# S5 parameters in one go at the beginning, and layer 0's S5 pieces issued from the second v product on

## The chip, the cores and the metric

The kernel runs on one core of a Trainium2 chip. The metric is the device time of one execution in microseconds (us); lower is better.

## The reference

A bidirectional encoder of two layers over a sequence of 512 tokens with 1024 channels. Each layer has three mixers that read one normed input `h`, a gated merge of them, and an MLP:

```python
for l in range(DEPTH):
    h = rmsnorm(x, g1)
    z = h @ w_in                    # 1024 -> all branches' columns
    ya = swish(g) * head_norm(retention_bidir(rotary(q), rotary(k), v))   # A: 4 heads
    yb = glu(gelu(s5_bidir(u)))     # B: 16 groups, 64 complex states, both directions
    yc = swish(g) * head_norm(gla_bidir(q, k, v, log_gate))               # C: 4 heads
    x += (sum of sigmoid(h @ w_m) * (y @ w_y)) @ w_out
    x += relu(rmsnorm(x) @ w1) ** 2 @ w2
```

The S5 branch is a diagonal complex state `s[n] = a * s[n-1] + b * u[n]` for each group and direction, with `a` and `b` worked out from learned Lambda, dt and B.

## The kernel before

Activations lie as 128 channels by 512 tokens. Weights come in chunks of 128x1024: a DMA brings `raw`, ScalarE copies the rounded part to `whi` (L111), VectorE subtracts for the rest, `wlo` (L112), and TensorE multiplies three times for each 128x128 block: `whi` by the activation's high part (L128), `whi` by its low part (L129), `wlo` by its high part (L130). For the v products the roles of the operands are exchanged (L393, L395, L397). A chunk is 24 matmuls of 512 columns or 48 of 256.

In layer 0 the program goes: u tiles, low-rank gate input `lrT` (L597 to L613), four q and k tiles of GLA (`zc`, L376), the four gates (`gla_gate`, L631 to L654: VectorE scans `cum`, ScalarE exponentials, GpSimd's small products `dec`), two v products of GLA, four rotary tiles of retention (`za`; GpSimd's product with the sine L747, VectorE's sum L749, TensorE's transposes L770), two v products of retention (centred at L758 and L759), and then the silu and gate tiles, 3 S5 pieces behind each. All of this is issued by generators. The foreground, `self.fg`, steps through the heads of GLA and retention behind each product; the background, `self.bg`, is stepped by `bg_steps`, which holds the new instructions behind given anchors (`issue_after`).

Instructions of each engine run in the order in which they stand in its queue, which a scheduling layer makes out of priorities (`hp`) and these anchors. An instruction that waits holds up everything behind it on its engine.

The S5 branch has three parts that matter here. `s5_params` works out, for all layers and directions at once, Lambda's exponentials and powers in some 185 small operations of 128x32 on GpSimd (L895 to L1010; the reciprocal L976 stands on VectorE). `s5_prep` fetches the tile `s5BC` with a DMA that GpSimd issues (L1021), builds the powers `s5V` (copied from the parameters at L1027 and L1028, doubled at L1092 to L1099), `s5Bb` (L1035 to L1037), `W` (L1056 to L1061), TensorE's small products `psK` (L1070), `s5X` (L1116 to L1118), and transposes it on TensorE (L1125). `s5_half` multiplies (L1163, L1212) and scans (L1182).

Of the kernel before, what the change touches and what calls it, by code (L numbers as in the profile page):

```python
# [40 lines left out]
class Hybrid:  # L41
# [181 lines left out]
    def run(self):  # L223
        nc, io = self.nc, self.io
        self.cst = self.one([P, 2432], "cst")
        xp = [self.sb.tile([P, 2, 512], F32, tag="xp", bufs=4, name=self.nm("xp")) for _ in range(KT // 2)]
        self.x = [xp[j // 2][:, j % 2, :] for j in range(KT)]
        self.chunk = 0
        self.pre = {}
        with self.hp(25000):  # L230
            nc.sync.dma_start(self.cst[:, C_SM:C_N], io["cst"][:, C_SM:])
            nc.sync.dma_start(self.x[0], io["xT"][:, 0, :])
            self.prefetch(0, 0, 2)
            nc.sync.dma_start(self.x[1], io["xT"][:, 1, :])
            nc.sync.dma_start(xp[1], io["xT"][:, 2:4, :])
            self.prefetch(0, 1, 2)
            for j in (2, 3):
                nc.sync.dma_start(xp[j], io["xT"][:, 2 * j:2 * j + 2, :])
            nc.sync.dma_start(self.cst[:, 0:C_MB], io["cst"][:, 0:C_MB])
        nc.sync.dma_start(self.cst[:, C_MB:C_SM], io["cst"][:, C_MB:C_SM])  # L240
        self.xsrc = [io["xT"][:, j, :] for j in range(KT)]
        self.sm = self.cst[:, C_SM:C_N]
        self.ident = self.cst[:, C_ID:C_ID + P]
        self.ones = self.cst[:, C_ONE:C_ONE + P]

        zero, warm = self.slot(s="warm"), self.ms()
        with self.hp(40000):
            nc.vector.memset(zero, 0.0)
            for _ in range(3):
                nc.tensor.matmul(warm, zero[:, 0:P], zero, start=True, stop=True)  # L250
        self.warm = lambda: nc.tensor.matmul(warm, zero[:, 0:P], zero, start=True, stop=True)
        accs, h = [], []
        with self.hp(35000):
            for j in range(KT):
                h.append(self.scaled_split(self.x[j], self.sm[:, SM_G1 + j:SM_G1 + j + 1]))
        with self.hp(30000):
            for j in range(KT):
                self.acc_sq(accs, self.x[j], j, nc.vector)
        self.params = self.s5_params()
        next(self.params)  # L260
        for l in range(self.depth):
            self.chunk = 0
            h, accs = self.layer(l, h, accs)
# [160 lines left out]
    def layer(self, l, h, acc):  # L424
        nc, io = self.nc, self.io
        r, R, _ = self.norm_stats(acc)
# [14 lines left out]
                        lst.append(d)  # L441
        with self.hp(8000):
            gl = [self.gla_gate(hd, lrT, qd[hd], kd[hd]) for hd in range(4)]
        G, gla_o, cv = [], [], []
        for hd in range(4):
            G.append(self.gla_work(hd, qd[hd], kd[hd], gl[hd], cv, gla_o))
        cv.append(self.v_tiles(l, h, r, lambda: None))
        self.fg(G[0])
        cv.append(self.v_tiles(l, h, r, lambda: self.fg(G[0], G[1])))
        self.fg(G[0], G[1])  # L450
        aq, ak, av, ret_o = [], [], [], []
        cs, sn = self.slot(s="cos"), self.slot(s="sin")
        with self.tc.issue_after(self.wdma.ins):
# [2 lines left out]
        for t, lst, gens in ((0, aq, (G[1], G[2])), (0, ak, (G[2], G[3])), (1, aq, (G[2], G[3])), (1, ak, (G[3],))):  # L456
            z = self.z_tile(l, h, R, "za")
            with self.hp(10000):
                lst.append(self.rotary(z, cs, sn))
            self.fg(*gens)  # L460
        if l == 0:
            with self.tc.issue_after(self.rot[0].ins), self.tc.issue_after(self.rot[1].ins):
                next(self.params, None)
        Q = [self.ret_work(t, aq, ak, av, ret_o) for t in range(2)]
        av += self.center(self.v_tiles(l, h, r, lambda: self.fg(Q[0])))
        self.fg(Q[0], Q[1])
        yb = []
        self.bg = self.s5_work(l, us, yb)
        n = 3 if l == 0 else 1

        def silu(*gens):
# [78 lines left out]
        self.bg = iter(())  # L550
        prep = []
        if l + 1 < self.depth:
            self.bg = (None for t in range(2) for _ in self.s5_prep(l + 1, t, prep))
        acc, hn = [], []
        for q in range(4):
            hid = []
# [457 lines left out]
    def s5_prep(self, l, t, res):  # L1014
# [34 lines left out]
        for d in range(2):  # L1049
            k0 = kb + d * 4  # L1050
            sl = slice(0, 5) if d == 0 else slice(4, None, -1)
            pb = [self.pw[:, ri, k0:k0 + 4, sl].unsqueeze(3).to_broadcast(sh) for ri in range(2)]
            cb = [C[:, ri, d * 4:d * 4 + 4, :].unsqueeze(2).to_broadcast(sh) for ri in range(2)]
            for ri in range(2):
                tw = self.part(sh, "w5t")
                e1.tensor_mul(w[d][ri], pb[0], cb[ri])  # L1056
                e1.tensor_mul(tw, pb[1], cb[1 - ri])
                if ri == 0:
                    e1.tensor_sub(w[d][0], w[d][0], tw)
                else:  # L1060
                    e1.scalar_tensor_tensor(f(w[d][1]), f(w[d][1]), -1.0, f(tw), ALU.mult, ALU.subtract)  # L1061
                yield
        psK = self.ms([P, 2, 64])
        for d in range(2):
            kw = 0 if d == 0 else 1
# [40 lines left out]
        for d in range(2):  # L1106
            k0 = kb + d * 4
            sh = [P, 4, 4, 16]
            sl = slice(3, None, -1) if d == 0 else slice(0, 4)
            pb = [self.pw[:, ri, k0:k0 + 4, sl].unsqueeze(3).to_broadcast(sh) for ri in range(2)]  # L1110
            bb = [Bb[:, ri, d * 4:d * 4 + 4, :].unsqueeze(2).to_broadcast(sh) for ri in range(2)]
            PT = self.slot(shape=(P, 2, 2, P), s="s5PT" + z)
            X = self.slot(shape=(P, 2, 4, 4, 16), s="s5X")
            tx = self.slot(shape=(P, 1, 4, 4, 16), s="s5tx")
            for ri in range(2):
                e1.tensor_mul(X[:, ri], pb[0], bb[ri])  # L1116
                e1.tensor_mul(tx[:, 0], pb[1], bb[1 - ri])
                (e1.tensor_sub if ri == 0 else e1.tensor_add)(X[:, ri], X[:, ri], tx[:, 0])  # L1118
            nc.scalar.copy(d8[:, d], self.r4[:, k0:k0 + 4].unsqueeze(2).to_broadcast([P, 4, P]))
            e2.memset(d8[:, d, :, 0 if d == 0 else P - 1], 0.0)  # L1120
            yield
            pst = self.ms([P, 2, 2, P])
            for ri in range(2):
                for h in range(2):
                    nc.tensor.transpose(pst[:, ri, h, :], X[:, ri, 2 * h:2 * h + 2].rearrange("p a b c -> p (a b c)"),  # L1125
                                        self.ident)
            nc.scalar.copy(PT, pst)
            PTs.append(PT)
            yield
        res.append((w, M, Vr, Vi, PTs, d8))  # L1130

    def bg_steps(self, n, *anchors):

        with ExitStack() as st:
            for a in (*anchors, self.pool):
                st.enter_context(self.tc.issue_after(a.ins))
            for _ in range(n):
                next(self.bg, None)

    def s5_work(self, l, us, yb):  # L1140

# [7 lines left out]
    def s5_half(self, l, t, uU, prep, yb):  # L1149
# [6 lines left out]
        for d in range(2):  # L1156
# [37 lines left out]
                for x in S:  # L1194
                    e2.memset(x[:, :, 0 if d == 0 else P - 1], 0.0)
            Sp.append(S)
            yield

        Y = self.slot(shape=(P, 4, P), s="s5Y")
        psm = self.ms([P, 4, P])  # L1200
# [154 lines left out]
```

## Time and profile before

| what | value |
|---|---|
| median of 3 runs | 1555.6 us (1554.44 to 1556.1) |
| the profiled execution's own time | 1557.27 us |
| its span, first to last instruction | 1555.3 us |
| TensorE busy in it | 1536.5 us, 99% |
| VectorE busy | 950.2 us, 61% |
| ScalarE busy | 560.7 us, 36% |
| GpSimd busy | 214.4 us, 14% |
| TensorE's mean granted clock | 0.997 of full speed |

The span is the time from the first to the last instruction of one profiled execution; the execution's own time is 2 us longer. The profiled execution is 0.1% above the median. Busy shares are averages over the whole span.

### The profile page before, as it was taken

To read this page: it belongs to the slowest core of one execution; us is meant where nothing else is said; L and a number is where in the kernel's file an instruction comes from. 1 tells how busy PE (TensorE), PEld (TensorE's weight loads), DVE (VectorE), ACT (ScalarE), POOL (GpSimd) and SP (SyncE) were. 2 spreads that over 40 slices of the span, in tenths; PEclk is the share of its full clock that TensorE was granted. 3 is DMA by queue.
4 is the path that set the end of the run, shared out by engine and by line. 5 is a ranking of instruction groups with operands and counts; after the bars stand their busy time and mean duration, and the time that the engine had idled before them with its cause. 6 is when DMAs were issued, how large, how long until landed. Compare 5 with 4: busy or idle time off the path is not lost.

```text
span 1555.3 us, 20304 instructions
## 1 busy us (share of the span) xinstructions
PE 1536.5 (99%) x7984; PEld 1284.0 (83%) x7984; DVE 950.2 (61%) x1570; ACT 560.7 (36%) x842; POOL 214.4 (14%) x319
## 2 busy tenths in 40 slices
PE   8999999999999999999999999999999999999998
PEld 6988877888888888888889888888888888888897
DVE  6878999745655757434558788594466534343352
ACT  4534243324443232423435333233343413233242
POOL 8225010232200000000101211123121000000001
PEclk9999999999999999999999999999999999999999
DMA  6623223233332314231435222233332332223221
GB/s 211 190 62 109 67 82 114 97 112 130 109 102 76 125 55 141 86 111 61 142 118 161 89 89 82 91 113 122 109 135 95 98 106 95 95 95 105 85 95 54
DMA packets 59342, 163.86 MB, mean 105 GB/s; under 512 B 10540, under 2 KB 15148, under 8 KB 59248
## 3 DMA queue, kind: packets, MB, share of 16 engines
q1 hardware_dynamic: 58784, 161.27, 31.5%
q8 instruction: 62, 1.02, 0.3%
q0 software_dynamic: 320, 1.05, 0.3%
q14 instruction: 32, 0.26, 0.1%
q10 hardware_dynamic: 144, 0.26, 0.0%
HBM read 147.64 MB, written 6.52 MB: 99 GB/s over the span
## 4 chain that ended last, share of the span: by engine, by line
PE 86%; DVE 8%; DMA 2%; POOL 1%; issue 1%; SPq 1%; ACT 0%; DVEq 0%; POOLq 0%; ACTq 0%
PE mm L128 26%; PE mm L129 26%; PE mm L130 26%; DVE wlo L112 1%; DMA rsw<-za 1%; PE mm L393 1%; PE mm L395 1%; PE mm L397 1%; SPq L746 1%; PE mm L307 1%; DMA xp<-xT 0%; PE m L1163 0%; PE ms L673 0%; POOL sp L895 0%; PE m L1212 0%
## 5 line engine op out<-in xcount | busy, mean ns | idle before, releaser
L128 PE MATMUL mm<-hh,whi 128*128 128x512 f32 x1136 | 446.4, 393 | 0.4 <-ACT v L406 0.4
L130 PE MATMUL mm<-hh,wlo 128*128 128x512 f32 x1136 | 444.1, 391 | 0.8 <-DVE wlo L112 0.8
L129 PE MATMUL mm<-hl,whi 128*128 128x512 f32 x1136 | 444.1, 391 | 0.0
L111 ACT CAST whi<-raw 128x1024 fp32r<-128x1024 f32 (+1 forms) x250 | 258.3, 1041 | 223.2 <-PE mm L130 161.0
L112 DVE TENSOR_TENSOR wlo<-raw,whi 128x1024 fp32r<-128x1024 f32 (+1 forms) x250 | 329.4, 1318 | 3.7 <-PE mm L129 2.5
L128 PEld LDWEIGHTS mm<-hh,whi 128*128 128x128 f32 x1136 | 213.7, 188 | 46.6 <-issue 1.8
L130 PEld LDWEIGHTS mm<-hh,wlo 128*128 128x128 f32 x1136 | 213.6, 188 | 45.7 <-DVE wlo L112 1.2
L129 PEld LDWEIGHTS mm<-hl,whi 128*128 128x128 f32 x1136 | 213.7, 188 | 45.0 <-issue 1.6
L129 PE MATMUL mm<-fl,whi 128*128 128x512 f32 x448 | 174.4, 390 | 0.0
L130 PE MATMUL mm<-fh,wlo 128*128 128x512 f32 x448 | 174.1, 389 | 0.0
L128 PE MATMUL mm<-fh,whi 128*128 128x512 f32 x448 | 173.5, 390 | 0.0
L576 DVE TENSOR_TENSOR x<-x,mm 128x512 f32<-128x512 f32 x56 | 38.5, 687 | 134.8 <-PE mm L130 134.8
L563 ACT ACTIVATE ht<-ht 128x512 f32<-128x512 f32 x64 | 40.4, 632 | 186.8 <-DVE ht L562 186.8
L562 DVE SCALAR_TENSOR_TENSOR ht<-mm,R 128x512 f32<-128x512 f32 x64 | 44.2, 690 | 103.5 <-PE mm L130 92.5
L213 POOL TENSOR_TENSOR acc<-acc,sq 128x512 f32<-128x512 f32 (+1 forms) x24 | 30.6, 1275 | 551.4 <-ACT sq L212 551.4
L128 PEld LDWEIGHTS mm<-fh,whi 128*128 128x128 f32 x448 | 84.1, 188 | 17.8
L130 PEld LDWEIGHTS mm<-fh,wlo 128*128 128x128 f32 x448 | 84.1, 188 | 17.5
L129 PEld LDWEIGHTS mm<-fl,whi 128*128 128x128 f32 x448 | 84.1, 188 | 17.3
L490 ACT ACTIVATE g<-g,cst 128x512 f32<-128x512 f32 x48 | 34.8, 724 | 163.0 <-DVE g L489 163.0
L117 DVE TENSOR_TENSOR fl<-ht,fh 128x512 fp32r<-128x512 f32 x64 | 44.3, 692 | 71.6 <-ACT fh L116 71.6
L489 DVE TENSOR_TENSOR g<-mm,R 128x512 f32<-128x512 f32 x48 | 33.0, 687 | 63.3 <-PE mm L130 63.3
L130 PE MATMUL mm<-y,wlo 128*128 128x512 f32 x160 | 62.7, 392 | 0.9 <-DVE wlo L112 0.9
(297 smaller groups left out, 2134.4 us busy)
## 6 DMA issues: line engine op xcount, KB each, us to landing
raw<-wst SPq DMA_DIRECT2D x254, 512.0 KB, 3.3
dup<-zc SPq DMA_DIRECT2D x32, 128.0 KB, 3.5
rsw<-za SPq DMA_DIRECT2D x32, 64.0 KB, 2.3
qfb<-za SPq DMA_DIRECT2D x16, 128.0 KB, 2.3
x<-xT SPq DMA_DIRECT2D x8, 256.0 KB, 3.7
xs<-x SPq DMA_DIRECT2D x8, 256.0 KB, 2.4
x<-xs SPq DMA_DIRECT2D x8, 256.0 KB, 3.8
xp<-xT SPq DMA_DIRECT2D x3, 512.0 KB, 8.9
```

Source lines behind the costliest of these rows:

```text
L111: nc.scalar.copy(hi[:, s], raw[:, s])
L112: nc.vector.tensor_sub(lo[:, s], raw[:, s], hi[:, s].bitcast(F32))
L117: self.nc.vector.tensor_sub(lo, src, hi.bitcast(F32))
L128: nc.tensor.matmul(ps, hi[:, o:o + P], a, start=first and k == 0, stop=False)
L129: nc.tensor.matmul(ps, hi[:, o:o + P], b, start=False, stop=False)
L130: self.mmi = nc.tensor.matmul(ps, lo[:, o:o + P], a, start=False, stop=last and k == n - 1)
L213: return (eng or (nc.vector if j == KT - 1 else nc.gpsimd)).tensor_add(accs[0], accs[0], t)
L489: ev = nc.vector.tensor_mul(g, ps, R)
L490: act = nc.scalar.activation(g, g, AF.Sigmoid, bias=self.smc(l, SM_BM, j))
L562: ev = nc.vector.scalar_tensor_tensor(t, ps, 0.0, R2, ALU.max, ALU.mult)
L563: act = nc.scalar.square(t, t)
L576: ev = nc.vector.tensor_add(self.x[j], self.x[j], ps)
```

## The change

The generator `s5_params` is run to its end at the start, where before its first half was issued there and its second half behind the four rotary tiles. The background of S5 is set up behind the gates, and in layer 0 one step of it is taken behind each foreground step from the second v product on, with TensorE's last matmul and GpSimd's last product of the gates as anchors. The step count behind silu and gate tiles stays 3, but a step that yields a true value, which stands where the next piece begins on TensorE, ends the round. Lines of the changed kernel are those of before plus 1 (L376 is L377), plus 5 (L640 to L1125 are L645 to L1130), or plus 7 (L1163, L1212 and L1226 are L1170, L1219 and L1233). The work is the same; no instruction of the computation is added or taken away.

```diff
--- before.py
+++ after.py
@@ -257,7 +257,8 @@
             for j in range(KT):
                 self.acc_sq(accs, self.x[j], j, nc.vector)
         self.params = self.s5_params()
-        next(self.params)
+        for _ in self.params:
+            pass
         for l in range(self.depth):
             self.chunk = 0
             h, accs = self.layer(l, h, accs)
@@ -441,13 +442,22 @@
                         lst.append(d)
         with self.hp(8000):
             gl = [self.gla_gate(hd, lrT, qd[hd], kd[hd]) for hd in range(4)]
+        yb = []
+        self.bg = self.s5_work(l, us, yb)
+        self.pool = gl[0][1]
+
+        def fg(*gens):
+            self.fg(*gens)
+            if l == 0:
+                self.bg_steps(1, self.mmi)
+
         G, gla_o, cv = [], [], []
         for hd in range(4):
             G.append(self.gla_work(hd, qd[hd], kd[hd], gl[hd], cv, gla_o))
         cv.append(self.v_tiles(l, h, r, lambda: None))
         self.fg(G[0])
-        cv.append(self.v_tiles(l, h, r, lambda: self.fg(G[0], G[1])))
-        self.fg(G[0], G[1])
+        cv.append(self.v_tiles(l, h, r, lambda: fg(G[0], G[1])))
+        fg(G[0], G[1])
         aq, ak, av, ret_o = [], [], [], []
         cs, sn = self.slot(s="cos"), self.slot(s="sin")
         with self.tc.issue_after(self.wdma.ins):
@@ -457,15 +467,10 @@
             z = self.z_tile(l, h, R, "za")
             with self.hp(10000):
                 lst.append(self.rotary(z, cs, sn))
-            self.fg(*gens)
-        if l == 0:
-            with self.tc.issue_after(self.rot[0].ins), self.tc.issue_after(self.rot[1].ins):
-                next(self.params, None)
+            fg(*gens)
         Q = [self.ret_work(t, aq, ak, av, ret_o) for t in range(2)]
-        av += self.center(self.v_tiles(l, h, r, lambda: self.fg(Q[0])))
-        self.fg(Q[0], Q[1])
-        yb = []
-        self.bg = self.s5_work(l, us, yb)
+        av += self.center(self.v_tiles(l, h, r, lambda: fg(Q[0])))
+        fg(Q[0], Q[1])
         n = 3 if l == 0 else 1
 
         def silu(*gens):
@@ -550,7 +555,7 @@
         self.bg = iter(())
         prep = []
         if l + 1 < self.depth:
-            self.bg = (None for t in range(2) for _ in self.s5_prep(l + 1, t, prep))
+            self.bg = (x for t in range(2) for x in self.s5_prep(l + 1, t, prep))
         acc, hn = [], []
         for q in range(4):
             hid = []
@@ -1059,7 +1064,7 @@
                     e1.tensor_sub(w[d][0], w[d][0], tw)
                 else:
                     e1.scalar_tensor_tensor(f(w[d][1]), f(w[d][1]), -1.0, f(tw), ALU.mult, ALU.subtract)
-                yield
+                yield d and ri
         psK = self.ms([P, 2, 64])
         for d in range(2):
             kw = 0 if d == 0 else 1
@@ -1118,7 +1123,7 @@
                 (e1.tensor_sub if ri == 0 else e1.tensor_add)(X[:, ri], X[:, ri], tx[:, 0])
             nc.scalar.copy(d8[:, d], self.r4[:, k0:k0 + 4].unsqueeze(2).to_broadcast([P, 4, P]))
             e2.memset(d8[:, d, :, 0 if d == 0 else P - 1], 0.0)
-            yield
+            yield 1
             pst = self.ms([P, 2, 2, P])
             for ri in range(2):
                 for h in range(2):
@@ -1126,16 +1131,18 @@
                                         self.ident)
             nc.scalar.copy(PT, pst)
             PTs.append(PT)
-            yield
+            yield d
         res.append((w, M, Vr, Vi, PTs, d8))
 
     def bg_steps(self, n, *anchors):
+
 
         with ExitStack() as st:
             for a in (*anchors, self.pool):
                 st.enter_context(self.tc.issue_after(a.ins))
             for _ in range(n):
-                next(self.bg, None)
+                if next(self.bg, None):
+                    break
 
     def s5_work(self, l, us, yb):
 
@@ -1194,7 +1201,7 @@
                 for x in S:
                     e2.memset(x[:, :, 0 if d == 0 else P - 1], 0.0)
             Sp.append(S)
-            yield
+            yield 1
 
         Y = self.slot(shape=(P, 4, P), s="s5Y")
         psm = self.ms([P, 4, P])
```

How this moves instructions is seen in the engines' queues. First VectorE, behind the low-rank input `lrT` in layer 0. `wlo_527` of before and `wlo_574` of the change are the same chunk, the sixth counted from 0 (chunk 5). Before:

```order
L610 TENSOR_TENSOR lrT_392<-lrt_394,lrT_392 32x512
L112 TENSOR_TENSOR wlo_527<-raw_524,whi_526 128x1024
L376 TENSOR_TENSOR zc_477<-mm_452,R_277 128x512
L640 SCALAR_TENSOR_TENSOR a_565<-ms_563,a_565 128x512
L642 SCALAR_TENSOR_TENSOR cum_571<-scm_401,a_565 64x512
L643 SCALAR_TENSOR_TENSOR cum_571<-scm_401,a_565 64x512
```

With the change:

```order
L615 TENSOR_TENSOR lrT_439<-lrt_441,lrT_439 32x512
L1032 COPY s5V_145_921<-cst 128x8
L1033 COPY s5V_146_922<-cst 128x8
L1098 TENSOR_TENSOR s5V_145_921<-s5V_145_921 128x8
L1097 TENSOR_TENSOR s5vt_1611<-s5V_146_922 128x8
L1103 TENSOR_TENSOR s5V_146_922<-s5V_146_922,s5V_145_921 128x8
L1099 TENSOR_TENSOR s5V_145_921<-s5V_145_921,s5vt_1611 128x8
L1102 TENSOR_TENSOR s5vt_1611<-s5V_145_921,s5V_146_922 128x8
L112 TENSOR_TENSOR wlo_574<-raw_571,whi_573 128x1024
L1098 TENSOR_TENSOR s5V_145_921<-s5V_145_921 128x8x2
```

Two copies from the parameters `cst` and five products of `s5V` now stand ahead of the chunk's `wlo`, and more of them follow behind it.

Second GpSimd, behind the end of the parameters' first part. Before, the gate's `dec` follows it directly:

```order
L926 TENSOR_TENSOR sp_179<-sp_179 128x32
L904 TENSOR_SCALAR sp_222<-sp_222 128x32
L904 TENSOR_SCALAR sp_179<-sp_179 128x32
L653 TENSOR_TENSOR dec_581<-a_565,e_96_574 64x3
L654 TENSOR_TENSOR dec_581<-a_565,e_96_574 64x3
L685 MEMSET st_841 64x128
L686 MEMSET st_841 64x128
```

With the change (`sp`, `pwt` and `cst` are tiles of the parameters):

```order
L1013 TENSOR_TENSOR pwt_279<-cst 128x64
L900 TENSOR_TENSOR sp_253<-sp_253 128x32 x2
L1015 TENSOR_TENSOR cst<-pwt_278,pwt_279 128x32x2
L1014 TENSOR_TENSOR cst<-pwt_278,pwt_279 128x32x2
L900 TENSOR_TENSOR cst<-sp_253,sp_222 128x32 x2
L658 TENSOR_TENSOR dec_628<-a_612,e_99_621 64x3
L659 TENSOR_TENSOR dec_628<-a_612,e_99_621 64x3
L1026 DMA s5BC_917<-s5bc 128x512
L690 MEMSET st_888 64x128
L691 MEMSET st_888 64x128
```

The rest of the parameters now stands ahead of `dec`, of which these are the last rows, and the DMA of `s5BC` (L1021 before) stands right behind `dec`. The copies of `s5V` on VectorE wait for the last of the powers `v4r`, `v4i` and `r4`, which is the 135th instruction of GpSimd's queue, counted from its start; before, the 101st and 102nd were the L926 products of which one is shown above.

Third VectorE in the second half of layer 0's S5, around the last transposes of `s5X`. Before:

```order
L1116 TENSOR_TENSOR s5X_2734<-cst,s5Bb_2402 128x256 x2
L117 TENSOR_TENSOR y_3466<-yb_2358,y_3465 128x512
L112 TENSOR_TENSOR wlo_2874<-raw_2871,whi_2873 128x1024
L502 TENSOR_TENSOR g_2590<-g_2590,mm_2801 128x512
L1118 TENSOR_TENSOR s5X_2734<-s5X_2734,s5tx_2735 128x256
L1117 TENSOR_TENSOR s5tx_2735<-cst,s5Bb_2402 128x256
L1118 TENSOR_TENSOR s5X_2734<-s5X_2734,s5tx_2735 128x256
L1169 TENSOR_TENSOR s5a_2815<-m_459_2784,s5V_392_2398 128x2x2x128
```

With the change:

```order
L1121 TENSOR_TENSOR s5X_2734<-cst,s5Bb_2402 128x256 x2
L117 TENSOR_TENSOR y_3466<-yb_2358,y_3465 128x512
L1123 TENSOR_TENSOR s5X_2734<-s5X_2734,s5tx_2735 128x256
L112 TENSOR_TENSOR wlo_2874<-raw_2871,whi_2873 128x1024
L507 TENSOR_TENSOR g_2590<-g_2590,mm_2801 128x512
L1122 TENSOR_TENSOR s5tx_2735<-cst,s5Bb_2402 128x256
L1123 TENSOR_TENSOR s5X_2734<-s5X_2734,s5tx_2735 128x256
L1176 TENSOR_TENSOR s5a_2815<-m_459_2784,s5V_387_2364 128x2x2x128
```

The sum L1118 (L1123 now) on the first half of `s5X` stood behind the chunk's `wlo_2874` and a gate's product, and now stands ahead of both.

## Rows read from the trace of the kernel before

**Rows 1.** Stretches: from:to, length, busy us of PE, PEld, DVE, ACT, POOL, TensorE's clock.
```profile
40.00:72.00 32.00, 32.00 (x223) 29.39 (x222) 25.18 (x30) 19.68 (x34) 6.75 (x12) 1.00 0.74 214
72.00:120.00 48.00, 48.00 (x335) 43.05 (x334) 39.34 (x88) 18.90 (x56) 11.26 (x18) 1.00 0.25 70
268.00:270.00 2.00, 2.00 (x7) 1.68 (x6) 2.00 (x5) 1.40 (x2) 0.00 (x0) 0.50 0.09 33
```

**Rows 2.** TensorE's waits from 40 to 300: total, times, longest.
```profile
PE ms L1125 <- DVE s5X L1118: 2.0, 1, 2.0
PE mm L130 <- DVE wlo L112: 1.7, 2, 0.9
PE ms L770 <- DVE za L749: 1.3, 1, 1.3
PE ms L809 <- DVE v L759: 0.7, 1, 0.7
PE ms L738 <- DVE ro L836: 0.6, 1, 0.6
```

**Rows 3.** Timeline of TensorE, start and duration: one of the waits on wlo.
```profile
247.18 0.39 PE L129 MATMUL mm<-y,whi 128*128 128x512 f32 x1
248.46 0.50 PE L130 MATMUL mm<-y,wlo 128*128 128x512 f32 x1 [0.90 <-DVE wlo L112]
```

**Rows 4.** Timeline of TensorE behind the last wait: two matmuls at the low clock.
```profile
269.21 0.63 PE L128 MATMUL mm<-hh,whi 128*128 128x512 f32 x1
269.64 0.63 PE L129 MATMUL mm<-hl,whi 128*128 128x512 f32 x1
```

**Rows 5.** Timeline of GpSimd in the parameters, both parts, and dec between them.
```profile
30.72 0.47 POOL L913 TENSOR_TENSOR sp<-sp 128x32 f32<-128x32 f32 x2
...
39.30 0.29 POOL L904 TENSOR_SCALAR sp<-sp 128x32 f32<-128x32 f32 x1
39.55 1.88 POOL L926 TENSOR_TENSOR sp<-sp 128x32 f32<-128x32 f32 x2
...
51.30 0.69 POOL L653 TENSOR_TENSOR dec<-a,e 64x3 f32<-64x3 f32 x1 [9.37 <-DVE dup L650]
52.06 1.07 POOL L654 TENSOR_TENSOR dec<-a,e 64x3 f32<-64x3 f32 x1
...
130.04 0.24 POOL L895 TENSOR_TENSOR sp<-sp 128x32 f32<-128x32 f32 x1
...
132.22 0.25 POOL L1007 TENSOR_TENSOR pwt<-cst 128x32 f32<-128x32 f32 x1
```

**Rows 6.** Timeline of VectorE: the chunk's wlo, a gate's sum and scan.
```profile
40.08 1.22 DVE L112 TENSOR_TENSOR wlo<-raw,whi 128x1024 fp32r<-128x1024 f32 x1
...
44.19 0.69 DVE L640 SCALAR_TENSOR_TENSOR a<-ms,a 128x512 f32<-128x512 f32 x1 [2.28 <-ACT a L639]
44.91 1.22 DVE L642 TENSOR_TENSOR_SCAN cum<-scm,a 64x512 f32<-64x512 f32 x1
```

**Rows 7.** Timeline of VectorE: operations of the S5 pieces, in their old place.
```profile
140.94 0.29 DVE L1035 TENSOR_TENSOR s5Bb<-s5BC,cst 128x128 f32<-128x128 f32 x1
...
141.75 0.49 DVE L1056 TENSOR_TENSOR W<-cst,s5BC 128x320 f32<-128x320 f32 x1
...
162.68 0.17 DVE L1092 TENSOR_TENSOR s5vt<-s5V 128x8 f32<-128x8 f32 x1
```

**Rows 8.** Timeline of TensorE: the first use of wlo in chunk 5, 6, 8.
```profile
46.82 0.39 PE L130 MATMUL mm<-hh,wlo 128*128 128x512 f32 x1
47.05 0.39 PE L128 MATMUL mm<-hh,whi 128*128 128x512 f32 x1
...
51.92 0.28 PE L395 MATMUL mm<-wlo,hh 128*128 128x256 f32 x1
...
64.49 0.28 PE L395 MATMUL mm<-wlo,hh 128*128 128x256 f32 x1
```

**Rows 9.** The tile s5BC, four DMAs: from issue to landing.
```profile
DMA to landing us min/median/max: 2.9/3.0/4.7
```

## The prediction

> **What bounds the kernel now.** I began with the table of busy times: TensorE is busy in 99% of the span, so only its few pauses can be given back, and every new one is paid. The busy time by stretches [rows 1] shows where none are: from 40 to 72 us TensorE is busy in 32.00 of 32.00 us, from 72 to 120 in 48.00 of 48.00. VectorE is busy in 25.18 and 39.34 us there, so it idles for 6.8 and 8.7 us; this is the room into which the change moves S5 work.
>
> Then TensorE's own waits [rows 2]: six of them between 40 and 300 us, 2.0 + 1.7 + 1.3 + 0.7 + 0.6 = 6.3 us, every one for VectorE. The reader should see that none is for a DMA or for GpSimd, though these stand one step further back. A pause costs somewhat more than its idle time: around one wait for a `wlo` the starts are 248.46 - 247.18 = 1.28 us apart [rows 3] where the normal spacing is 47.05 - 46.82 = 0.23 [rows 8], so 1.05 are lost where the wait says 0.90. With 0.15 for each of six, 0.9 more. Behind the last wait the clock is granted at half [rows 1], and the matmuls start 0.43 us apart [rows 4] instead of 0.23. Some eight of them make 8 x 0.20 = 1.6 us. So 6.3 + 0.9 + 1.6 = 8.8 us is what the change can win at most here. Everything behind 300 us keeps its order, but for one small operation of VectorE.
>
> **The change part by part.** The edits change no work, so the sum is of new pauses against old ones.
>
> *A first new wait, in chunk 5.* VectorE's queue now holds the copies of `s5V` and five products ahead of chunk 5's `wlo`. They need the powers that GpSimd writes with its 135th instruction; before, 100 were behind it when the 101st began at 39.55 us [rows 5]. So 35 are left. Their pace: 34 instructions in 39.30 - 30.72 = 8.58 us, 0.25 each, or 11 in 132.22 - 130.04 = 2.18 us, 0.20 each [rows 5]. Dependent products and plain ones are mixed in both, so I take the middle: the powers are there at 39.55 + 35 x 0.227 = 47.5 us (46.6 to 48.4). VectorE, which in the old trace began this `wlo` at 40.08 [rows 6], has by its queue nothing else to do until then. Seven small operations follow; one takes 0.17 us [rows 7], less where the next one overlaps it, so I put 0.14 on each, 1.0 in all, and the `wlo` takes 1.22 [rows 6]. It ends at 49.7 us. TensorE uses it at 46.82 [rows 8]. **Term 1: +2.9 us.** Lower end, at 0.20 and 0.1 each, 1.7. Upper end: the pair at 39.55 took 1.88 us instead of 0.5 while VectorE worked [rows 5]; three more such pairs would add 4.1 and give 7.
>
> *The rule that bears on this pace.* Those two products took 0.94 us each beside VectorE's operations, against 0.20 to 0.25 elsewhere [rows 5]. The Trainium skill's SBUF — State Buffer (Who interferes with whom) says that a VectorE instruction with two SBUF inputs contends with a GpSimd instruction that reads SBUF, and holds it up. By that rule GpSimd would run free while VectorE stands still for it, the pace would be the 0.20 of the quiet stretch, and term 1 would be 2.0 instead of 2.9, the sum 0.9 us lower. The trace agrees as to the slow pair, but 34 instructions at 0.25 with a largely idle VectorE keep me at the middle.
>
> *A second, in chunk 6.* Behind chunk 5's `wlo` stand 13 small `s5V` operations (1.8), a `zc` and a gate's sum at 0.7 each, two scans of 1.22 [rows 6], then chunk 6's `wlo`: 49.7 + 1.8 + 1.4 + 2.4 + 1.2 = 56.5 us. TensorE, 2.9 late, wants it at 51.92 [rows 8] + 2.9 = 54.8. **Term 2: +1.7 us.**
>
> *A third, in chunk 8.* GpSimd issues the DMA of `s5BC` right behind the gate's `dec`, and `dec` needs VectorE's difference behind the `zc` of chunk 6 (56.5 + 1.3 = 57.8) and two exponentials, which I put at an operation of VectorE each (0.65): 59.1. `dec` took 53.13 - 51.30 = 1.8 us [rows 5], so the DMA is issued at 60.9 and lands 3.0 later (2.9 to 4.7) [rows 9], at 63.9. VectorE holds the `s5Bb` products behind that wait, and behind these chunk 8's `wlo`: six of `s5Bb` at 0.2 from start to start, six of `W` at 0.4 (their durations are 0.29 and 0.49 [rows 7], with some overlap), a gate's sum 0.7, two scans 2.4, the `wlo` 1.2, in all 8 us: 71.9. TensorE wants it at 64.49 [rows 8] + 4.6 = 69.1. **Term 3: +2.8 us** (1.5 with a fast `dec`, 4.5 with a landing of 4.7).
>
> *Clock.* Three pauses of 2 to 3 us come where there were none; the one of 2.0 before went with a low clock. Behind the first, the wait in chunk 6 would cover it, since VectorE decides there. Behind the third it would cost 1.6. I take half, **+0.8**.
>
> *The later chunks.* The remaining products of `W` and `s5Bb`, about 4 us, fall into the stretch with 8.7 us of room [rows 1], and TensorE is 7.4 us later itself. I cost them at nothing; without that cover each us of VectorE is a us.
>
> *What is given back.* The `s5X` sums no longer stand behind a chunk's `wlo`: the 2.0 of L1125 and its clock go. VectorE no longer waits for parameters at 131 and 141, the rotary sum stands ahead of the chunk's `wlo`, and the small `s5V` operations of the first half lie a hundred us earlier: 1.3 and 0.6 go. The two waits for `wlo` lay behind work of the second half that now comes earlier: 1.7. Of the 0.7 at v's centring about half stays, as `psK` moves in between the two v halves; and one pause of some 0.5 at the S5 output products is likely to be new, as they come sooner behind their scans. **Returned: 8.8 - 0.4 - 0.5 = 7.9.**
>
> *Sum:* 2.9 + 1.7 + 2.8 + 0.8 - 7.9 = +0.3 us. On the profiled execution, 1557.3, this is 1557.6; on the median of 1555.6, 0.1% below it, **1555.9**.
>
> **The rivals.**
>
> *Faster: the early waits are short.* Term 1 at 1.7, a quick `dec` and no low clock make 1.7 + 1.7 + 1.5 = 4.9, and all 8.8 come back: -3.9, 1551.7 us. For it: GpSimd runs beside an idle VectorE. Against it: three terms must be at their low ends together.
>
> *Slower: the late waits stay.* VectorE gives up some 12 us of work between 130 and 270 us, but it still holds wide scans, products and every `wlo`; a wait removed may come back one chunk on. If only half of 8.8 returns, 7.4 + 0.8 - 4.4 = +3.8, 1559.4 us; with a second low clock 1561. It decides from a return below 5.1. For it: every wait of [rows 2] is for VectorE, and the change takes no work from it. Against it: in [rows 2] five places alone hold all.
>
> *Slower: GpSimd is held up.* At the upper end of term 1, 4 us more, the lateness is carried through chunks 6 and 8: +4.3, 1559.9 us; with the slow landing 1561.6. Against it: VectorE has nothing to hold GpSimd up with while it waits.
>
> *The change does nothing* is no case: the copies' place in the queue is certain, so some wait must come.
>
> **How the numbers follow.** A measurement of this kernel tells 0.2%, 3.1 us, from no change. The forecast, a wash within that, gets 0.42; the short early waits 0.25; late waits that stay 0.21, GpSimd held up 0.12. So faster 0.25, same 0.42, slower 0.33. The range must reach into both sides: down to 1550.5, the faster case with another us from a `wlo` that isn't late; up to 1563, the slower cases with a low clock more.
>
> **What would show it.** In the changed profile VectorE should idle from about 40 to 47.5 us for GpSimd, ahead of an `s5V` copy; TensorE should wait near 47 us for 2 to 4 us at L130, near 55 and near 69 at L395, and the windows from 40 to 72 should no longer be full. Around 265 there should be no wait at L1130 and no low clock. The transposes of `za` should not wait. Wrong would be: no early pause at all (the powers ready before 43), or the same five places waiting as before, or a pause of over 10 us in the first 100.

## The result, and the profile after

The changed kernel takes 1568.56 us (median of 4, 1566.66 to 1570.4), the kernel before 1555.35 (4 runs, 1554.44 to 1556.1): a recorded ratio of 1.0075, with a 95% interval of 1.0062 to 1.0088 (the two medians alone give 1.0085). It is 13 us slower, above the range of 1550.5 to 1563. The profiled execution of the change took 1566.66 us and is the fastest of its four; against the 1557.27 of before that is 9.4 us, and it is these that the trace can explain.

TensorE's waits in the changed kernel from 30 to 320 us, in the columns of [rows 2]:

```profile
PE mm L130 <- DVE wlo L112: 4.5, 1, 4.5
PE m L1219 <- DVE s5S L1198: 4.3, 2, 2.3
PE mm L394 <- ACT v L407: 4.0, 1, 4.0
PE mm L394 <- DVE za L377: 1.3, 1, 1.3
```

Not one of the five places of [rows 2] waits as before: L1125 (now L1130), L770, L809, L738 and the two waits at L130 near 225 and 247 us are gone. In their place stand 4.5, 4.0, 1.3 and, at the S5 output products L1219, 4.3 us in two waits.

The stretches that were full [rows 1], and three short ones, in the columns of that group:

```profile
40.00:72.00 32.00, 25.91 (x152) 22.44 (x151) 19.42 (x45) 9.38 (x15) 15.77 (x55) 0.95 0.53 147
72.00:120.00 48.00, 45.59 (x320) 41.06 (x321) 42.93 (x84) 25.09 (x58) 9.02 (x20) 0.96 0.35 105
50.00:55.00 5.00, 4.15 (x11) 3.30 (x12) 4.83 (x17) 0.00 (x0) 1.89 (x5) 0.66 0.36 82
75.00:80.00 5.00, 5.00 (x32) 5.00 (x31) 4.78 (x10) 4.51 (x8) 1.50 (x2) 0.66 0.85 270
222.00:226.00 4.00, 4.00 (x17) 2.99 (x18) 2.31 (x5) 2.14 (x3) 0.00 (x0) 0.58 0.35 131
```

From 40 to 72 us TensorE is busy in 25.91 us instead of 32.00, from 72 to 120 in 45.59 instead of 48.00. In the last three rows the granted clock is 0.58 to 0.66: part of each stretch ran at 1.2 GHz instead of 2.4, and each lies behind a pause of 2.3 to 4.5 us.

The first pause, on VectorE (start, duration, instruction, and in brackets the idle time ahead with what ended it):

```profile
38.73 0.83 DVE L615 TENSOR_TENSOR lrT<-lrt,lrT 32x512 fp32r<-32x512 f32 x1
47.97 0.19 DVE L1032 COPY s5V<-cst 128x8 f32<-128x8 f32 x1 [8.40 <-POOL cst L900]
...
49.45 1.34 DVE L112 TENSOR_TENSOR wlo<-raw,whi 128x1024 fp32r<-128x1024 f32 x1
...
66.48 0.29 DVE L1040 TENSOR_TENSOR s5Bb<-s5BC,cst 128x128 f32<-128x128 f32 x1 [3.59 <-DMA s5BC<-s5bc]
```

This is where the prediction looked: `lrT` at 38.73, then 8.40 us of nothing until GpSimd's powers let the copies of `s5V` go at 47.97, then the `wlo` of chunk 5 from 49.45 to 50.79. The same on TensorE:

```profile
45.99 0.39 PE L129 MATMUL mm<-hl,whi 128*128 128x512 f32 x1
50.85 0.50 PE L130 MATMUL mm<-hh,wlo 128*128 128x512 f32 x1 [4.47 <-DVE wlo L112]
...
51.97 0.63 PE L130 MATMUL mm<-hh,wlo 128*128 128x512 f32 x1
52.39 0.63 PE L128 MATMUL mm<-hh,whi 128*128 128x512 f32 x1
```

L130 starts 4.86 us behind L129 instead of 0.23, and the matmuls behind it are 0.42 us apart. The second pause is put down to ScalarE, whose queue the prediction hadn't followed; its timeline, TensorE's, and the row of GpSimd and the one of VectorE on which it hangs:

```profile
70.27 0.60 ACT L1047 COPY s5Bd<-s5Bb 64x128 f32<-64x128 f32 x2 [6.29 <-DVE s5Bb L1042]
72.58 0.21 ACT L651 ACTIVATE e<-cum 128x4 f32<-128x4 f32 x1 [1.71 <-DVE cum L648]
72.91 0.60 ACT L1047 COPY s5Bd<-s5Bb 64x128 f32<-64x128 f32 x2
73.52 0.84 ACT L407 ACTIVATE v<-mm,ny 128x256 f32<-128x256 f32 x2
```

```profile
69.92 0.48 PE L678 MATMUL ms<-dup,dup 64*128 64x128 f32 x2
74.41 0.39 PE L394 MATMUL mm<-whi,hh 128*128 128x256 f32 x1 [4.01 <-ACT v L407]
74.64 0.28 PE L396 MATMUL mm<-wlo,hh 128*128 128x256 f32 x1
```

```profile
62.29 0.77 POOL L1026 DMA_DIRECT2D s5BC<-s5bc  x1
```

```profile
73.19 1.22 DVE L112 TENSOR_TENSOR wlo<-raw,whi 128x1024 fp32r<-128x1024 f32 x1
```

ScalarE idles 6.29 us for `s5Bb`, which VectorE can't build before `s5BC` has landed (issued at 62.29, and 3.59 us of VectorE's waiting end at 66.48, above). The copies of `s5Bd` (L1047) and the gate's exponential stand in ScalarE's queue ahead of L407, which empties the v product's PSUM tile, and without that tile, free at 74.36, TensorE can't begin the next v product. But the `wlo` of the same chunk, chunk 8, stands behind the same DMA in VectorE's queue and ends at 73.19 + 1.22 = 74.41: by these rows, had ScalarE been in time, TensorE would have stopped one matmul later, at L396, until the same moment. The third kind of pause, at 220 us, on VectorE and TensorE:

```profile
220.53 0.69 DVE L1194 TENSOR_TENSOR s5e<-s5e,s5V 128x512 f32<-128x512 f32 x1 [1.17 <-POOL s5d L1125]
221.14 0.68 DVE L1198 TENSOR_TENSOR s5S<-s5a,s5b 128x508 f32<-128x508 f32 x1
```

```profile
219.25 0.40 PE L128 MATMUL mm<-hh,whi 128*128 128x512 f32 x1
221.97 0.70 PE L1219 MATMUL m<-s5S,W 64*64 64x128 f32 x8 [2.32 <-DVE s5S L1198]
...
223.62 0.63 PE L128 MATMUL mm<-hh,whi 128*128 128x512 f32 x1
```

The output products L1219 need `s5S` (L1198), for which VectorE itself has waited 1.17 us for GpSimd, and they are now only seven matmuls behind the first of their kind at 217. Before, 40 matmuls stood between the first and the next (L1212 there):

```profile
217.73 0.67 PE L1212 MATMUL m<-s5S,W 64*64 64x128 f32 x16
...
228.68 1.85 PE L1212 MATMUL m<-s5S,W 64*64 64x128 f32 x48
```

### The profile page after: what moved, and what is told of

Same layout as the page of the kernel before. It is cut to its first block, busy times and chain, and to the rows that moved or that the text cites. A ratio compares the mean times of both kernels' runs of the same rounds, so it can differ in the third digit from the quotient of the medians.

```text
span 1564.8 us, 20298 instructions
## 1 busy us (share of the span) xinstructions
PE 1539.8 (98%) x7984; PEld 1286.3 (82%) x7984; DVE 949.3 (61%) x1570; ACT 560.3 (36%) x842; POOL 206.2 (13%) x319
## 4 chain that ended last, share of the span: by engine, by line
PE 88%; DVE 6%; POOL 3%; DMA 1%; issue 1%; SPq 1%; ACT 0%; DVEq 0%; POOLq 0%; ACTq 0%
PE mm L128 26%; PE mm L129 26%; PE mm L130 26%; PE mm L394 1%; DVE wlo L112 1%; PE mm L398 1%; PE mm L396 1%; DMA rsw<-za 1%; PE mm L308 1%; POOL sp L917 1%; SPq L751 1%; PE ms L678 1%; PE m L1219 0%; PE m L1170 0%; PE ms L832 0%
## 5 line engine op out<-in xcount | busy, mean ns | idle before, releaser
L130 PE MATMUL mm<-hh,wlo 128*128 128x512 f32 x1136 | 444.6, 391 | 4.5 <-DVE wlo L112 4.5
L129 PE MATMUL mm<-hl,whi 128*128 128x512 f32 x1136 | 444.8, 392 | 0.0
L130 PEld LDWEIGHTS mm<-hh,wlo 128*128 128x128 f32 x1136 | 214.0, 188 | 49.9 <-DVE wlo L112 5.3
L129 PEld LDWEIGHTS mm<-hl,whi 128*128 128x128 f32 x1136 | 214.1, 188 | 45.0 <-issue 1.6
L129 PE MATMUL mm<-fl,whi 128*128 128x512 f32 x448 | 174.4, 390 | 0.0
L130 PE MATMUL mm<-fh,wlo 128*128 128x512 f32 x448 | 174.1, 389 | 0.0
L129 PEld LDWEIGHTS mm<-fl,whi 128*128 128x128 f32 x448 | 84.1, 188 | 17.5
L130 PEld LDWEIGHTS mm<-fh,wlo 128*128 128x128 f32 x448 | 84.1, 188 | 17.4
L128 PE MATMUL mm<-y,whi 128*128 128x512 f32 x160 | 62.7, 392 | 0.0
```

The costliest lines, as they stand in the source:

```text
L128: nc.tensor.matmul(ps, hi[:, o:o + P], a, start=first and k == 0, stop=False)
L129: nc.tensor.matmul(ps, hi[:, o:o + P], b, start=False, stop=False)
L130: self.mmi = nc.tensor.matmul(ps, lo[:, o:o + P], a, start=False, stop=last and k == n - 1)
```

## The experiments

The ratios below are to the kernel before, measured beside each run (medians of 1555.3 to 1556.2 us). Names in the edits are those of the changed kernel.

**e1_params: only the parameters in one go.**

```diff
 (kernel before)
         self.params = self.s5_params()
-        next(self.params)
+        for _ in self.params:
+            pass
```

> Only the first part of the change: the parameters run to their end at the beginning, S5's pieces stay behind the silu and gate tiles. Theory A (the loss comes from VectorE's and ScalarE's queues, where early S5 pieces wait for GpSimd's powers and for the DMA of s5BC): nothing of VectorE's stands behind the parameters early, so no pause of TensorE between 40 and 120 us, and the two waits of VectorE at 131 and 141 us go: 1553 to 1556 us. Theory B (the loss comes from GpSimd being busy with parameters when the gates' dec are due): slower than before, 1559 us or more.

1552.68 us, ratio 0.998 (0.997 to 0.9989). Theory B falls: the parameters that GpSimd now works out earlier are in nobody's way, and this part of the change wins 2.6 us. VectorE's waits from 120 to 150 us show it, first before, then here; those for the parameters at L976 and L1027 are gone:

```profile
DVE sp L976 <- POOL sp L895: 1.7, 1, 1.7
DVE s5V L1027 <- POOL cst L895: 1.6, 1, 1.6
```

```profile
DVE za L749 <- DMA rsw<-za: 2.8, 1, 2.8
```

**e2_nobreak: the change without the rule that ends a round.**

```diff
-                if next(self.bg, None):
-                    break
+                next(self.bg, None)
```

> The changed kernel without the rule that a piece that begins on TensorE ends the round of steps. Theory A: the early waits stay as they are, 1565 to 1570 us. Theory C (the loss is that the pieces now come out in smaller rounds, so that the S5 output products stand too close behind their scans and wait for them): these waits go, 1560 to 1564 us.

1564.39 us, ratio 1.0055 (1.0035 to 1.0076), between the two expectations. Both theories hold in part: the early pauses are there, and the long waits at the output products are not (none of them is over 0.3).

```profile
PE mm L130 <- DVE wlo L112: 5.0, 2, 3.6
PE mm L394 <- ACT v L407: 4.4, 1, 4.4
PE mm L396 <- DVE wlo L112: 1.7, 1, 1.7
```

**e4_anchor: the early steps behind the chunk's `wlo`.**

```diff
-                nc.vector.tensor_sub(lo[:, s], raw[:, s], hi[:, s].bitcast(F32))
+                self.wsub = nc.vector.tensor_sub(lo[:, s], raw[:, s], hi[:, s].bitcast(F32))
...
-                self.bg_steps(1, self.mmi)
+                self.bg_steps(1, self.mmi, self.wsub)
```

> The changed kernel, with VectorE's last wlo as one more anchor for the early single steps, so that VectorE's part of a piece stands behind the wlo of the chunk whose weights were last fetched; nothing else. The copies of s5V then stand behind the wlo of chunk 8 instead of ahead of that of chunk 5. Theory A: the pauses at 46 and 70 us go and their low clocks with them, 12 us less than the changed kernel by its profile: 1554 to 1559 us. Theories B and C: GpSimd's work and the rounds are the same, so 1565 us or more.

1559.86 us, ratio 1.0025 (1.0016 to 1.0035): 8.7 us less than the change, just above what theory A gave. The pause for the powers is gone and that at L394 down to 0.3, but new ones stand in the GLA heads, which I had not expected:

```profile
PE m L1219 <- DVE s5S L1198: 4.3, 2, 2.3
PE ms L702 <- DVE st L697: 3.8, 2, 2.5
PE ms L678 <- DVE sT L681: 1.4, 1, 1.4
PE mm L394 <- ACT v L407: 0.3, 1, 0.3
```

**e5_bcfirst: the change, with layer 0's first `s5BC` fetched at the beginning.**

```diff
+        self.bc0 = self.pslot(shape=(P, 2, 2, 8, 16), s="s5BC")
+        self.nc.gpsimd.dma_start(self.bc0, self.io["s5bc"][0, 0])
         self.params = self.s5_params()
...
```

In `s5_prep` this tile then takes the place of the one fetched there.

> The changed kernel, with the DMA of s5BC for layer 0's first half issued at the very beginning, ahead of the parameters. Theory A: the wait for the powers at 46 us stays with its low clock (6 us), the second at 70 us (4 us, and a low clock) goes: 1561 to 1565 us. If the second wait is ScalarE's own and not owed to s5BC: 1566 to 1570 us, with the wait for the v tile still there.

1563.56 us, ratio 1.0054 (1.0035 to 1.0072), 5.0 us less, as theory A says. The 4.0 at L394 has gone; 1.4 and 2.4 us at the GLA products L680 remain of that stretch.

**e6_anchor_nobreak: e4_anchor and e2_nobreak together.** Edit: both diffs.

> e4_anchor without the rule that ends a round ahead of a piece that begins on TensorE. Theory A (early S5 work of VectorE and ScalarE in front of the work that TensorE wants next, wherever it stands) leaves the waits of the GLA heads at 73, 81 and 110 us in place, 5 to 6 us; theory C in its part (the round ends bring the S5 output products too close behind their scans) takes the two waits of 2.3 and 2.0 us and a low clock away: 1554 to 1556.5 us. If the rounds don't matter: 1559 to 1561 us.

1558.72 us, ratio 1.0017 (1.0006 to 1.0028), 2 us above the expectation. The waits at the output products shrink from 4.3 to 0.3 us, those of the GLA heads stay (3.8 and 0.9), and a wait of 1.4 for a `wlo` near 207 us is new. Against e4_anchor only 1.1 us are won.

**e7_params_break: parameters and rule, no early steps.** Every `fg` of the change is `self.fg` again:

```diff
-        cv.append(self.v_tiles(l, h, r, lambda: fg(G[0], G[1])))
+        cv.append(self.v_tiles(l, h, r, lambda: self.fg(G[0], G[1])))
...
```

> Parameters in one go and the rule that ends a round, but no early steps: S5's pieces behind the silu and gate tiles, as before. Against e1_params (1552.7 us) it has the rule alone more. Theory C: the output products wait for their scans, 2 waits of 2 us: 1555 to 1558 us. If the rule only moves waits from one piece to another: 1551 to 1554 us.

1551.55 us, ratio 0.9976 (0.9965 to 0.9987). The rule alone costs nothing here: 1.1 us less than e1_params, within what the intervals allow, so the time that theory C gave is not reached. But a wait of its kind is there: one of 2.7 us at L1219 is nearly all that is left from 30 to 320 us:

```profile
PE m L1219 <- DVE s5S L1198: 2.7, 1, 2.7
```

**e8_late and e9_rotary: early steps that begin later, behind the `wlo`, without the rule.** The first steps stay `self.fg` up to the last v product (e8) or up to the first rotary tile (e9).

> Parameters in one go, early single steps only at the last v product (retention's), two of them, behind the chunk's wlo on VectorE, and rounds of 3 without the rule. Theory A: GLA's heads are through by then, so no wait of theirs; the late waits (223, 260, 286 us in e1_params, some 3 us) move or shrink: 1550 to 1553 us. If early pieces cost wherever they stand: 1554 us or more.

> As e8_late, but single steps from the first rotary tile on, six of them. Theory A: the pieces fall among the last GLA heads and hold their state products up, by part of the 6 us of e4_anchor: 1553 to 1557 us. If only the waits for parameters and s5BC count (both are over by then): 1550 to 1553 us.

1552.48 us, 0.9978 (0.9969 to 0.9987), and 1553.75 us, 0.9991 (0.9982 to 1.0001). With e1_params (no early step, 1552.68) and e6_anchor_nobreak (eight, from the second v product, 1558.72) they make a series. No difference among the first three is clear of the intervals, so late steps win nothing; the two steps that e6_anchor_nobreak has more than e9_rotary, ahead of the rotary tiles, cost 5.0 us.

**e10_gap: e7_params_break, with an empty round ahead of the output products.**

```diff
             Sp.append(S)
             yield 1
 
+        if l == 0:
+            yield 1
         Y = self.slot(shape=(P, 4, P), s="s5Y")
```

> e7_params_break with one empty round more in layer 0, between the last scan of an S5 half and its output products. In e7_params_break these products wait 2.7 us for their scans and a short low clock follows; theory C: a tile more in between hides the wait, 1547 to 1550 us. If the wait only moves to what now comes last: 1551 to 1553 us.

1549.02 us, ratio 0.996 (0.9945 to 0.9975), the fastest of all. The wait at the output products is gone, and the longest left is 0.7:

```profile
PE ms L775 <- DVE ny L144: 0.7, 1, 0.7
```

**e11_late_break: e8_late with the rule.** Edit: the rule of the change is kept.

> e8_late with the rule that ends a round. Without early steps the rule was worth 1 us (e7_params_break against e1_params), with eight early steps it cost 1 to 4. If two late single steps don't matter to it: 1550.5 to 1552.5 us. If the rule costs where pieces come earlier: 1553 us or more.

1552.2 us, ratio 0.998 (0.9971 to 0.999): no difference from e8_late. Without the steps ahead of the rotary tiles the rule is neutral.

**e12_moreparams: the change, with 20 more operations of GpSimd.**

```diff
         c = ts(cm, 1.0, ALU.add)
+        for _ in range(20):
+            e.tensor_scalar(c, c, 0.0, None, ALU.add)
         yield
```

> The changed kernel with 20 more small operations of GpSimd in the parameters, each of which adds zero. By this the scheduling layer puts the copies of s5V behind the wlo of chunks 5 and 6 instead of ahead of that of chunk 5. Theory A (the place in VectorE's queue decides): the pause at 46 us and its low clock go, though GpSimd has 4 to 5 us more to do; a shorter wait stays ahead of chunk 7, and the one at 70 us stays: 1561 to 1566 us. Theory B (GpSimd's time decides): 4 us slower than the changed kernel, 1570 us or more.

1566.62 us, ratio 1.0068 (1.0047 to 1.009). It is not the 4 us slower of theory B, and by the intervals no different from the change, but not as theory A said either. The copies stand behind two more chunks' `wlo`, and VectorE waits for the powers there instead, longer, and one pause of 9.0 us takes the place of two:

```profile
DVE s5V L1034 <- POOL cst L900: 10.9, 1, 10.9
```

```profile
PE mm L396 <- DVE wlo L112: 9.0, 1, 9.0
```

So the place decides which chunk is late, and GpSimd's time how long. Neither alone gives the size.

**e13_nowprod, e14_anchor_bcfirst, e15_bcfirst_nowprod: what holds the GLA heads up.** All three start from e6_anchor_nobreak. e13 leaves the `W` products of layer 0's first half out and sets `W` to zero, e14 fetches the first `s5BC` at the beginning (the diff of e5), e15 does both.

```diff
+                if kb == 0:
+                    e2.memset(w[d][ri], 0.0)
+                    yield d and ri
+                    continue
                 tw = self.part(sh, "w5t")
```

> e6_anchor_nobreak, with the W products of layer 0's first S5 half left out and W set to zero by GpSimd instead: 12 operations of VectorE of 0.4 us, 4.9 us, less, between 70 and 110 us. Theory A (VectorE's S5 work in front of the products of the GLA states is what TensorE waits for at 73, 81 and 110 us): these waits shrink from 4.7 us to under 2, 1554 to 1556.5 us. If those waits are owed to something else (GpSimd's memsets, the DMA of s5BC): 1558 to 1560 us.

> e6_anchor_nobreak (1558.7 us) with the DMA of s5BC for layer 0's first half issued at the very beginning; VectorE's order is the same. Theory D (VectorE's wait for that DMA, in front of the second gate's sum and scans, starts the lateness of the GLA heads): the wait of 1.8 us at 66 us goes and the waits at 73 to 123 us shrink by as much or more: 1555 to 1557 us. Theory E (the work of VectorE alone, 7 us of it in a stretch with 8.7 us of room, all told): 1558 to 1559.5 us.

> e14_anchor_bcfirst with the W products of the first half left out and W set to zero by GpSimd, so that neither the wait nor most of the work is left. Theories D and E together: the waits at 73 to 123 us go to under 1.5 us in all: 1552.5 to 1555 us. If a third thing holds the heads up: 1557 us or more.

1559.7 us (ratio 1.0028, 1.0016 to 1.0039), 1556.22 us (1.0001, 0.9992 to 1.001) and 1554.43 us (0.9982, 0.9973 to 0.9992). e13 missed: without the products the kernel is no faster. In its trace VectorE waits 3.4 us for `s5BC` where e6_anchor_nobreak waits 1.8, and the rotary tile `za` is later too, so a transfer and the work are mixed there. e14 answers to theory D, with 2.5 us won. With the wait gone the work shows: e15 wins another 1.8. TensorE's waits in the last two; in both, 0.8 at L680 stays:

```profile
PE ms L704 <- DVE st L699: 2.8, 2, 2.5
...
```

```profile
PE mm L130 <- DVE wlo L112: 1.4, 1, 1.4
PE mm L396 <- DVE za L379: 1.4, 1, 1.4
...
```

**e16_all: the change with the anchor, the early `s5BC` and the empty round.** Edit: the diffs of e4, e5 and e10.

> The change with three mends: VectorE's anchor, s5BC fetched at the beginning, and the empty round ahead of the output products. Against e10_gap (1549.0 us), which has the last and no early steps, it shows what early steps are worth when nothing of theirs waits: 1551 to 1555 us if VectorE's early work still costs, under 1549 us if the early place was right and only the waits were wrong.

1551.8 us, ratio 0.9971 (0.9959 to 0.9982). With the three mends the early steps still leave it 2.8 us above e10_gap, which has none (the intervals of the two ratios overlap, the runs do not). Not every wait is mended: two in the GLA heads stay, 2.9 us at L704 and 0.8 at L680, and behind the former the clock falls. In e10_gap the longest of the heads is 0.3, and TensorE is busy in 48.00 of the 48 us from 72 to 120. So what the early steps still cost stands in the heads; e15_bcfirst_nowprod, without the `W` products on VectorE, has no wait at L704.

```profile
PE ms L704 <- DVE st L699: 2.9, 2, 2.5
```

```profile
109.00:114.00 5.00, 3.82 (x18) 3.81 (x19) 4.33 (x7) 0.46 (x1) 0.88 (x3) 0.66 0.14 39
```

**e17_change_gap: the change with the empty round alone.** Edit: the diff of e10.

> The change itself with the empty round ahead of the output products and nothing else. Theory C for the loss behind 200 us: the two waits of 2.3 and 2.0 us and the low clock behind the first go, the early pauses stay: 1561 to 1565 us. If they only move: 1566 to 1570 us.

1560.49 us, ratio 1.0024 (1.0015 to 1.0034): 8.1 us less than the change, somewhat more than theory C gave. The 4.3 us at the output products go down to 0.4, and their low clock goes with them (1.00 from 222 to 226). These rows make some 5.5 of the 8.1 us; the rest stands in no wait of the trace.

```profile
PE m L1221 <- DVE s5S L1199: 0.4, 1, 0.4
```

## Why the prediction was wrong

**The account of the runs.** Parameters in one go: 1555.3 to 1552.7, a gain of 2.6 us. The rule on top: 1551.6. The early steps on top of both: 1568.6, a loss of 17.0. An empty round takes 8.1 us off the change and 2.5 off e7_params_break, which leaves 17.0 - 8.1 + 2.5 = 11.5 (rounded) between e17_change_gap and e10_gap, which differ in the early steps alone. Of the 11.5, VectorE's anchor and the early `s5BC` take off 8.7 together, with the waits for the powers and for `s5BC` and the low clocks behind them; the 2.8 us by which e16_all still exceeds e10_gap stand with the waits of the GLA heads. All of these are differences of medians, and the kernel before itself differs by up to 0.9 us from one measurement to another.

**Early pauses: the mechanism was right, the size was not.** The sum had 2.9 + 1.7 + 2.8 for the pauses and 0.8 for the clock, 8.2 us. The profile has waits of 4.5 and 4.0, and two low clocks, some 1.6 us each as before [rows 4]: behind the first, eight matmuls and more are 0.42 us apart instead of 0.23, behind the second 16 of 256 columns 0.21 instead of 0.12. That makes 11.7. Chunk 8's first `wlo` product shows it too: 64.49 before [rows 8], 74.64 here, 10.15 us later, with the second low clock still to come.

- *Term 1* (+2.9) measured 4.5. GpSimd's powers came at 47.9, where 47.5 was put; the seven small operations took 49.45 - 47.97 = 1.5 us instead of 1.0, with GpSimd at work beside them (0.17 to 0.39 us each; the products of the same lines took 0.17 to 0.19 from 51.8 on, when GpSimd had ended); and TensorE reached the place 0.6 us sooner. GpSimd's own pace beside the waiting VectorE was 30 instructions in 47.89 - 41.34 = 6.55 us, 0.22 each, and a pair of L931 took 0.46 us where one of the same line (L926 before) had taken 1.88 [rows 5].

```profile
41.34 0.46 POOL L931 TENSOR_TENSOR sp<-sp 128x32 f32<-128x32 f32 x2
...
47.89 0.44 POOL L900 TENSOR_TENSOR sp<-sp,cst 128x32 f32<-128x32 f32 x2
```

  The Trainium skill's SBUF — State Buffer (Who interferes with whom) says that VectorE's operations with two SBUF inputs contend with GpSimd's reads of SBUF. The trace agrees: at 41.34 VectorE had none under way, and the pair was quick. The pace of 0.22 was nearer the 0.20 of the quiet stretch than the 0.25, but the term came out larger for the other reasons.
- *Term 2* (+1.7) is not among the waits, because the low clock behind the first pause brought TensorE to chunk 6 just when its `wlo` was there. Where that clock stayed full, in e2_nobreak, the wait stands with 1.7 us, as forecast, and chunk 6 goes on at nearly the same time (e2_nobreak, then the change):

```profile
57.63 0.39 PE L396 MATMUL mm<-wlo,hh 128*128 128x256 f32 x1 [1.66 <-DVE wlo L112]
```

```profile
57.89 0.39 PE L396 MATMUL mm<-wlo,hh 128*128 128x256 f32 x1
```

  So the wait and this low clock are one cost and not two, as the prediction said under *Clock*. Terms 1 and 2 together measured 4.5 + 1.6 = 6.1 instead of 4.6.
- *Term 3* (+2.8) measured 4.0, within its bounds of 1.5 and 4.5, and the clock behind it fell whole, not by half (1.6 instead of 0.8). The path held: the DMA of `s5BC` was issued at 62.29 instead of 60.9, VectorE went on at 66.48 instead of 63.9, and the stretch from there to the end of chunk 8's `wlo`, put at 8 us, took 74.41 - 66.48 = 7.9. The missing part came from the DMA, issued 1.4 us later and longer in landing than the 3.0 put, less the 1.3 us by which TensorE came later itself. One thing was left out: the same piece puts copies of `s5Bd` into ScalarE's queue, ahead of the PSUM tile's release, and it is this release that the trace names. It came at 74.36, as good as together with the `wlo`, so by these rows it added nothing; e5_bcfirst, which removes the wait for `s5BC`, removes both.
- *Later chunks*, costed at nothing, show no wait in the change itself, where TensorE comes late anyway; without that cover they lie at the root of the waits of e4_anchor, e6_anchor_nobreak and e16_all in the GLA heads (2.8 of L704's 3.8 us stay with `s5BC` early, e14_anchor_bcfirst; none without the products as well, e15_bcfirst_nowprod). Room on VectorE in sum (8.7 us of 48) is no room where a chain of the heads wants it next.

**Returned: the step that failed most.** Of 8.8 us the sum kept 7.9. All the waits of [rows 2] did go, as it said. But "one pause of some 0.5 at the S5 output products" was mis-sized: it became two of 2.3 and 2.0 with a low clock behind the first, and a wait of 1.3 for a `za` tile is new: 4.3 + 1.6 + 1.3 = 7.2 us. What comes back is then 8.8 - 7.2 = 1.6, not 7.9. By these rows the change costs 11.7 - 1.6 = 10.1 us on the profiled execution, where 9.4 were measured; and 0.6 is won ahead of the first pause, which TensorE reaches that much sooner. That the output products' place is the cause is shown by e17_change_gap and e10_gap. It is the rule that ends a round which puts them there: without it (e2_nobreak) no wait of theirs is over 0.3 us, with it and without early steps (e7_params_break) one is 2.7.

**The rivals.** "The late waits stay" had the direction, and its condition, a return below 5.1, was met with 1.6; but its price (+3.8) is less than half of the 9.4 measured, and the old waits did not stay: new ones came at another place. "GpSimd is held up" is refuted: VectorE's wait ends at 47.97, near the forecast. The windows from 40 to 72 are no longer full and L1130 doesn't wait, both as forecast; the pause forecast at L395 near 55 us did not come, and the one near 69 came at 70.4, one matmul earlier, at L394.

**What stays open.** The medians differ by 13.2 us and the profiled executions by 9.4. The other three runs of the change took 1.2 to 3.7 us longer than the profiled one. Their mean granted clock was 0.993, where the profiled one had 0.995; 0.002 of 1566 us are 3.1 us (1.6 to 4.7, as both figures are rounded), so more time at the low clock can account for it. Where it lies no trace shows.

## What to carry to other kernels

When background work is moved forward, look at every engine's queue behind its first instruction: an instruction that must wait holds up the queue behind it, and the price is read at the operand that TensorE wants next (here a `wlo`, and a PSUM tile that ScalarE should have released). An anchor behind the `wlo` on VectorE took 8.7 us off here (e4_anchor); one on ScalarE was not tried. Follow each moved piece through all queues, its DMA and its copies too, before a stretch is counted as room. And a consumer on TensorE wants a tile's distance from its producer: one empty round won 2.5 us without early steps and 8.1 with them, while no early step won anything.

The version to keep is e10_gap: parameters in one go, the pieces where they were, rounds that end ahead of TensorE, and an empty round before the output products, at 0.996 (0.9945 to 0.9975) of the kernel before.

## What the runs showed of the hardware

The clock does not follow from the length of a pause alone. In the change a pause of 2.3 us at 220 us, among dense matmuls, was followed by half the clock (0.58 from 222 to 226, shown above). In e2_nobreak TensorE stood still for 3.6 us at L130 near 47 us, and the clock stayed full; in e17_change_gap it stood still for 4.1 us behind the same matmuls, and the clock fell. The stretch from 52 to 54 us in e17_change_gap, then in e2_nobreak (columns of [rows 1]):

```profile
52.00:54.00 2.00, 2.00 (x6) 1.52 (x6) 1.84 (x10) 0.00 (x0) 0.00 (x0) 0.50 0.51 117
```

```profile
52.00:54.00 2.00, 2.00 (x10) 1.65 (x10) 1.86 (x10) 0.00 (x0) 0.00 (x0) 1.00 0.56 128
```

Nor does a low clock always cost its 1.6 us. Behind the first pause of the change it cost next to nothing: chunk 6 went on at 57.89 us, and at 57.63 in e2_nobreak, whose clock stayed full but which then waited 1.66 us for the `wlo`. The price of a forecast pause therefore has some 1.6 us of play, unless the operand that TensorE wants next comes late as well.
